# Token scales turned on VectorE, and the residual's way out set back by twelve steps

## The chip, the cores and the metric

The program runs on one core of a Trainium2 chip. The metric is device time in microseconds for one execution of the whole program. The kernel before takes 2173.52 us, the median of three runs from 2171.97 to 2175.43.

## What is computed

Two decoder layers over 256 tokens of width 2048, all in float32. The first mixes tokens with a gated MLP, the second with forgetting attention, whose keys and values come from the residual after the first layer; each is followed by a feed-forward part of width 5632 with a short causal convolution.

```python
def rmsnorm(x, g):
    r = lax.rsqrt(jnp.mean(x * x, axis=-1, keepdims=True) + EPS)
    return (x * r) * g

h = x
h = h + chunked_gmlp(rmsnorm(h, a_norm), a_w_in, a_v_norm, a_w_s, a_b_s, a_w_out)
h = h + conv_ffn(rmsnorm(h, f_norm[0]), f_w_up[0], f_conv_w[0], f_conv_b[0], f_w_down[0])
k, v, c = fox_shared_kv(h, kv_norm, w_kvf, b_f, k_norm)
h = h + forgetting_attention(rmsnorm(h, b_norm), b_w_qg, q_norm, b_w_out, k, v, c)
h = h + conv_ffn(rmsnorm(h, f_norm[1]), f_w_up[1], f_conv_w[1], f_conv_b[1], f_w_down[1])
return rmsnorm(h, final_norm)
```

The factor `r` of each rmsnorm is one number per token. The kernel multiplies the residual by the gain alone, runs the matmul on that, and applies `r` to the product; these 256 factors are the token scales.

## The kernel before

**The weights' way.** Every weight matrix comes from DRAM in chunks of 128 x 1024 floats (512 KB). Class `Stream` loads a chunk into a tile `raw` on SP's queue (line 78), six chunks ahead of its use, and three chunks ahead splits it in two: ScalarE rounds it to `whi` (line 112), VectorE takes the remainder `wlo` (line 113). TensorE then makes three products for each true one: rounded with rounded, remainder with rounded, rounded with remainder. So each operand has a high and a low part; the activations' parts lie in `X1`, `X2` (in the trace `mlp_X` and `att_X`) and `H` (`ffn_H`). All these matmuls stand on line 226, in the helper `mm`.

**Two kinds of blocks.** In a feature block (`feat_block`) the weights are stationary and the activations stream, 256 tokens at a time. In a token block (`tok_blocks`, `seven_block`) the activations are stationary and the weights stream, mostly 256 columns at a time. The trace lists the streamed operand first, so token blocks read `whi,X` and feature blocks `X,whi`. There are four `whi` and four `wlo` tiles in turn, each 1024 + 64 floats long; weights start at the tile's start in feature blocks and 32 floats further in token blocks (`FEAT_AT, TOK_AT = 0, 32`). Two tiles that nothing uses, `spare` of 16 floats and `place` of 144, stand in the pools.

**Steps.** Work beside the matmuls is written as generators. `advance` takes each of them one `yield` further after every chunk that TensorE has been given, so a `yield` is one chunk, and the order on every engine's queue is the order in which this code runs. Nothing reorders it later.

**Token scales.** `token_sums` sums the squares, and `rsqrt` leaves the 256 scales in `rcol`, 128 partitions by 2. For products that have tokens along the free dimension they are also wanted as a row on every partition, `rB`. `token_rows` writes `rcol` to DRAM from GpSimd's queue, one element of four bytes at a time (line 359), and reads the row back to all partitions (line 363). It runs twice: key "a" near the start, in one piece, and key "b" at about 1029 us, in eight pieces each way with two yields after each.

**The residual's way out.** During attention the residual `h` isn't needed, and its place is used by other tiles. `kv_operand` first prepares the operand `att_X2` from `h`, a step for each of 16 parts, and then sends `h` to the DRAM tensor `kept` in eight transfers of 256 KB, one after every two steps (line 1042, on SP's queue, which also carries the weight loads). `heads`, the attention itself, demands that all eight have been issued; its tiles `parts_qk` and `parts_pv` lie where `h` was.

Of the kernel before, what the change touches and what calls it, by code (L numbers as in the profile page):

```python
# [10 lines left out]
F32 = mybir.dt.float32  # L11
# [6 lines left out]
P = 128  # L18
D = 2048
T = 256  # L20
# [168 lines left out]
def build(ctx, tc, d, out):  # L189
    nc = tc.nc  # L190
    ctx.enter_context(tc.manual_schedule())
    const = ctx.enter_context(tc.tile_pool(name="const", bufs=1))
    wpool = ctx.enter_context(tc.tile_pool(name="wpool", bufs=AHEAD + 1))
    small = ctx.enter_context(tc.tile_pool(name="small", bufs=1))
# [8 lines left out]
    X1 = const.tile([P, KD, 2 * T], F32R, name="X1")  # L203
    acc = const.tile([P, T], F32, name="acc")
    rB = const.tile([P, T], F32, name="rB")
    rcol = const.tile([P, 2], F32, name="rcol")
    ident = const.tile([P, P], F32, name="ident")
    ones = const.tile([P, 2], F32, name="ones")

# [8 lines left out]
    def misc_ps():  # L218
        return psum.tile([P, 512], F32, name="mp", tag="mp", bufs=2)

    def column(i):
        return col[:, i:i + 1]
# [99 lines left out]
    def prep(dst, kt, gain):  # L322

        g = column(gain + kt)
        nc.scalar.activation(dst[:, kt, :T], h[:, kt, :], AF.Copy, scale=g)
        nc.vector.scalar_tensor_tensor(dst[:, kt, T:], h[:, kt, :], g, dst[:, kt, :T].bitcast(F32),
                                       op0=OP.mult, op1=OP.subtract)
# [17 lines left out]
    def token_sums():  # L345

        between()
        mp = misc_ps()
        sum_tokens(mp, acc, True, True)
        v = small.tile([P, 2], F32, name="ts_v", tag="ts_v", bufs=2)  # L350
        nc.vector.tensor_scalar(v, mp[:, :2], 1.0 / D, EPS, op0=OP.mult, op1=OP.add)
        rsqrt(rcol, v, 2)

    def token_rows(key, pieces=1):

        way = dram.tile([1, T], F32, name=f"way_r{key}")
        n = P // pieces
        for i in range(0, P, n):
            nc.gpsimd.dma_start(way.rearrange("o (t p) -> p (o t)", t=2)[i:i + n], rcol[i:i + n])
            yield  # L360
            yield
        for i in range(0, P, n):
            nc.gpsimd.dma_start(rB[i:i + n], way[:1, :].to_broadcast([n, T]))
            if n < P:
                yield
                yield

    def token_scale():
        yield
        token_sums()  # L370
        yield
        yield from token_rows("b")
# [338 lines left out]
    def residual_prepared():  # L711

        for p in range(8):
            while state["added"] < 2 * (p // 2 + 1):
                yield
            for kt in (2 * p, 2 * p + 1):
                prep(X1, kt, C_BNORM)
            if p == 5:
                s.start(residual_squares())
            yield  # L720

    def residual_squares():

        for p in range(8):
            while state["added"] < 2 * (p // 2 + 1):
                yield
            sq = small.tile([P, 2, T], F32, name="sq", tag="sq", bufs=2)
            nc.scalar.activation(sq, h[:, 2 * p:2 * p + 2, :], AF.Square)
            yield
            if p == 0:  # L730
                nc.vector.tensor_tensor(acc, sq[:, 0, :], sq[:, 1, :], op=OP.add)
            else:
                for i in range(2):
                    nc.vector.tensor_tensor(acc, acc, sq[:, i, :], op=OP.add)
        yield
        token_sums()
        state["rows"] = True
        yield
        yield from token_rows("b", 8)

    def short_block(src, x, K, done):

# [87 lines left out]
    def warm_up(n):  # L830

        mp = misc_ps()
        for _ in range(n):
            nc.tensor.matmul(mp[:, :P], ident, ident, start=True, stop=True)  # L834

    def input_norm():
        for _ in range(3):
            yield
        for p in range(8):
            if p % 2 == 0:  # L840
                yield
            square_into_acc(p)
        yield
        token_sums()
        state["normed"] = True
        yield
        yield from token_rows("a")
# [148 lines left out]
    def att(key):  # L996
        ph.open("att")
        shape = {"X2": [P, KD, 2 * T], "q": [P, NH, T], "k": [P, 4, 8, 4, 32], "v": [P, 2, D],
                 "ccol": [P, 2, NH], "gain": [P, 1]}[key]
        return ph.keep(key, shape, F32R if key == "X2" else F32)  # L1000
# [29 lines left out]
    def kv_operand():  # L1030
        for _ in range(3):
            yield
        nc.vector.tensor_tensor(att("gain"), column(C_QNORM), column(C_KNORM), op=OP.mult)
        for kt in range(KD):
            while state["added"] < 2 * (kt // 4 + 1):
                yield
            prep(att("X2"), kt, C_KVNORM)
            yield
        for i in range(8):
            yield  # L1040
            yield
            nc.sync.dma_start(kept[:, 2 * i:2 * i + 2, :], h[:, 2 * i:2 * i + 2, :])
        state["kept"] = True

# [250 lines left out]
    def g_done(p):  # L1295
        def done(ps, both):
# [4 lines left out]
            while state["done"] < 2 * p + 2 or state["gates"] < p:  # L1301
# [20 lines left out]
    nc.gpsimd.memset(ident, 1.0)  # L1322
    nc.gpsimd.affine_select(ident, ident, pattern=[[-1, P]], compare_op=OP.is_equal, fill=0.0,
                            base=0, channel_multiplier=1)
    warm_up(9)

    v_blocks = [(d["a_in_v"][8 * blk:8 * blk + 8], v_done(blk)) for blk in range(4)]
# [12 lines left out]
    for blk in range(4):  # L1340
        seven_block(blk, d["down0"][22 * blk:22 * blk + 22], order_of(blk, 2, (8, 4)), *sums_apart(blk))

    s.then(at_mult=lambda: s.start(kv_operand()))
    tok_blocks([(d["b_q"][8 * blk:8 * blk + 8], head_norm("q", blk)) for blk in range(4)], lambda: X1,
               order=[(n, i) for i in range(3) for n in range(6)] + [(6, 0), (7, 0), (0, 3), (1, 3), (6, 1), (7, 1)]
# [89 lines left out]
```

## Time and profile before

| what | value |
|---|---|
| median of three runs | 2173.52 us (2171.97 to 2175.43) |
| the profiled execution | 2175.22 us, granted clock 0.998 |
| its span, from first to last instruction | 2173.5 us |
| DMA engines, by queue | q1 66.0%, q0 0.6%, q8 0.4% of 16 engines' span |
| moved | 455.73 MB, mean 210 GB/s |

The span is what the profile's rows add up to; the 1.7 us around it are start and end of the execution. In the rows below, PE is TensorE, PEld its loading of stationary operands, DVE VectorE, ACT ScalarE, POOL GpSimd, SPq the queue that issues most transfers. A busy TensorE only says that a matmul is in flight; matmuls overlap, so how fast it goes is seen from how many start in a stretch.

### The profile page before, as it was taken

To read this page: it belongs to the slowest core of one execution; us is meant where nothing else is said; L and a number is where in the kernel's file an instruction comes from. 1 tells how busy PE (TensorE), PEld (TensorE's weight loads), DVE (VectorE), ACT (ScalarE), POOL (GpSimd) and SP (SyncE) were. 2 spreads that over 40 slices of the span, in tenths; PEclk is the share of its full clock that TensorE was granted. 3 is DMA by queue.
4 is the path that set the end of the run, shared out by engine and by line. 5 is a ranking of instruction groups with operands and counts; after the bars stand their busy time and mean duration, and the time that the engine had idled before them with its cause. 6 is when DMAs were issued, how large, how long until landed. Compare 5 with 4: busy or idle time off the path is not lost.

```text
span 2173.5 us, 45433 instructions
## 1 busy us (share of the span) xinstructions
PE 2161.4 (99%) x18558; PEld 2145.2 (99%) x18558; DVE 1671.2 (77%) x2448; ACT 1222.2 (56%) x1709; POOL 31.9 (1%) x60
## 2 busy tenths in 40 slices
PE   9999999999999999999999999999999999999998
PEld 9999999999999999999999999999999999999998
DVE  6696687777777799998877886668777777779997
ACT  6665555555555555566445775445555555555555
POOL 0000000000000000000000100000000000000000
PEclk9999999999999999999999999999999999999999
DMA  8686566666666567777977777566866666665665
GB/s 314 191 247 201 192 196 195 187 201 188 200 191 197 183 197 228 220 231 206 256 244 249 238 229 231 187 205 198 267 194 194 190 199 191 198 190 189 204 204 165
DMA packets 161729, 455.73 MB, mean 210 GB/s; under 512 B 26816, under 2 KB 50256, under 8 KB 161136
## 3 DMA queue, kind: packets, MB, share of 16 engines
q1 hardware_dynamic: 159552, 448.87, 66.0%
q0 software_dynamic: 1504, 3.41, 0.6%
q8 instruction: 145, 2.38, 0.4%
q10 hardware_dynamic: 464, 0.55, 0.1%
q14 instruction: 64, 0.52, 0.1%
HBM read 434.91 MB, written 17.84 MB: 208 GB/s over the span
## 4 chain that ended last, share of the span: by engine, by line
PE 96%; DMA 2%; DVE 1%; SPq 0%; ACT 0%; issue 0%; POOL 0%; DVEq 0%; ACTq 0%; POOLq 0%
PE ps L226 94%; PE mp L226 1%; DMA raw<-b_q 1%; DMA att_rows<-way_q 0%; DMA way_q<-att_turned 0%; DVE wlo L113 0%; DMA raw<-kvf_k 0%; DMA raw<-kvf_ks 0%; SPq L1014 0%; PE mp L834 0%; PE mp L1282 0%; PE ps L1279 0%; ACT whi L112 0%; ACT sq L459 0%; DVE h_h L801 0%
## 5 line engine op out<-in xcount | busy, mean ns | idle before, releaser
L113 DVE TENSOR_TENSOR wlo<-raw,whi 128x1024 fp32r<-128x1024 f32 (+1 forms) x724 | 878.8, 1219 | 262.3 <-ACT whi L112 258.4
L112 ACT ACTIVATE whi<-raw 128x1024 fp32r<-128x1024 f32 (+1 forms) x724 | 762.0, 1057 | 554.5 <-PE ps L226 432.4
L226 PE MATMUL ps<-X,whi 128*128 128x256 f32 (+1 forms) x6466 | 823.7, 280 | 0.0
L226 PEld LDWEIGHTS ps<-X,whi 128*128 128x128 f32 x6466 | 775.3, 188 | 6.8
L226 PE MATMUL ps<-X,wlo 128*128 128x256 f32 x3328 | 445.0, 276 | 0.0
L226 PEld LDWEIGHTS ps<-X,wlo 128*128 128x128 f32 x3328 | 409.7, 188 | 1.7
L226 PE MATMUL ps<-whi,ffn_H 128*128 128x256 f32 (+1 forms) x2124 | 347.1, 277 | 0.0
L226 PEld LDWEIGHTS ps<-whi,ffn_H 128*128 128x128 f32 x2124 | 292.8, 188 | 0.7
L226 PE MATMUL ps<-wlo,ffn_H 128*128 128x256 f32 (+1 forms) x1060 | 220.6, 277 | 0.0
L226 PE MATMUL ps<-whi,X 128*128 128x256 f32 (+1 forms) x1272 | 213.7, 279 | 0.0
L226 PEld LDWEIGHTS ps<-whi,X 128*128 128x128 f32 x1272 | 180.4, 188 | 1.3
L226 PE MATMUL ps<-whi,att_X 128*128 128x256 f32 (+2 forms) x970 | 169.6, 290 | 2.0 <-ACT whi L112 2.0
L978 DVE SCALAR_TENSOR_TENSOR ffn_room<-ffn_room,col 128x255 f32<-128x255 f32 x352 | 161.9, 481 | 6.4
L226 PEld LDWEIGHTS ps<-wlo,ffn_H 128*128 128x128 f32 x1060 | 165.7, 188 | 0.2
L226 PEld LDWEIGHTS ps<-whi,att_X 128*128 128x128 f32 x970 | 139.8, 190 | 5.5 <-ACT whi L112 2.2
L226 PE MATMUL ps<-wlo,X 128*128 128x256 f32 (+1 forms) x634 | 140.6, 279 | 0.0
L410 DVE TENSOR_TENSOR ffn_room<-ps,rB 128x512 f32<-128x512 f32 x76 | 52.5, 691 | 114.2 <-PE ps L226 114.1
L974 ACT ACTIVATE ffn_room<-ffn_room,col 128x256 f32<-128x256 f32 x176 | 96.3, 594 | 53.4 <-DVE ffn_room L410 53.4
L226 PE MATMUL ps<-wlo,att_X 128*128 128x256 f32 (+2 forms) x476 | 108.4, 292 | 0.9 <-DVE wlo L113 0.8
L226 PEld LDWEIGHTS ps<-wlo,X 128*128 128x128 f32 x634 | 102.6, 188 | 0.4
L90 ACT ACTIVATE whi<-raw 128x768 fp32r<-128x768 f32 x54 | 45.8, 848 | 79.6 <-PE ps L226 58.7
L90 ACT ACTIVATE whi<-ffn_room 128x512 fp32r<-128x512 f32 x108 | 64.3, 627 | 32.1 <-PE ps L226 18.9
(237 smaller groups left out, 1692.9 us busy)
## 6 DMA issues: line engine op xcount, KB each, us to landing
raw<-up SPq DMA_DIRECT2D x352, 512.0 KB, 4.2
raw<-down SPq DMA_DIRECT2D x176, 512.0 KB, 4.3
raw<-a_in_u SPq DMA_DIRECT2D x32, 512.0 KB, 4.5
raw<-a_out SPq DMA_DIRECT2D x32, 512.0 KB, 4.1
raw<-b_q SPq DMA_DIRECT2D x32, 512.0 KB, 4.6
raw<-kvf_v SPq DMA_DIRECT2D x32, 512.0 KB, 5.1
raw<-b_g SPq DMA_DIRECT2D x32, 512.0 KB, 4.0
raw<-b_out SPq DMA_DIRECT2D x32, 512.0 KB, 4.3
```

What stands on the lines that cost most here:

```text
L90: self.nc.scalar.activation(hi[:, cols], src[:, cols], AF.Copy)
L112: self.nc.scalar.activation(h, raw, AF.Copy)
L113: self.nc.vector.tensor_tensor(l, raw, h.bitcast(F32), op=OP.subtract)
L226: nc.tensor.matmul(o, a, b, start=start, stop=stop, skip_group_check=True)
L410: nc.vector.tensor_tensor(a, src, rB[:, None, :].to_broadcast([P, 2, T]), op=OP.mult)
L974: nc.scalar.activation(c[:, m, :], a[:, m, :], AF.Identity, scale=w[2], bias=column(C_CONVB + l * 2 * KF + f))
L978: nc.vector.scalar_tensor_tensor(c[:, m, n:], a[:, m, :T - n], w[k], c[:, m, n:], op0=OP.mult, op1=OP.add)
```

## The change

`rcol` becomes the first two columns of a tile `scales` of 128 x 32, which GpSimd sets to zero at the start. VectorE turns it in blocks of 32 x 32 into a new tile `turned_r`, so that in each block the 32 scales of a token half lie in one partition, behind each other. Four transfers of 2 x 32 floats take them to DRAM, and one transfer brings the row back to all partitions. For key "b" that is 1 + 2 yields in place of 32. And `kv_operand` waits twelve more steps before the residual goes out, with three steps instead of two before each transfer.

```diff
-    rcol = const.tile([P, 2], F32, name="rcol")
+    scales = const.tile([P, 32], F32, name="scales")
+    rcol = scales[:, :2]
...
-    def token_rows(key, pieces=1):
+    def token_rows(key):
 
         way = dram.tile([1, T], F32, name=f"way_r{key}")
-        n = P // pieces
-        for i in range(0, P, n):
-            nc.gpsimd.dma_start(way.rearrange("o (t p) -> p (o t)", t=2)[i:i + n], rcol[i:i + n])
-            yield
-            yield
-        for i in range(0, P, n):
-            nc.gpsimd.dma_start(rB[i:i + n], way[:1, :].to_broadcast([n, T]))
-            if n < P:
-                yield
-                yield
+        turned = small.tile([P, 32], F32, name="turned_r", tag="turned_r")
+        nc.vector.transpose(turned, scales)
+        yield
+        for g in range(4):
+            nc.gpsimd.dma_start(way.rearrange("o (t g i) -> (o t) g i", t=2, g=4)[:, g, :],
+                                turned[32 * g:32 * g + 2, :])
+        yield
+        yield
+        nc.gpsimd.dma_start(rB, way[:1, :].to_broadcast([P, T]))
...
-        yield from token_rows("b", 8)
+        yield from token_rows("b")
...
             prep(att("X2"), kt, C_KVNORM)
             yield
+        for _ in range(12):
+            yield
         for i in range(8):
-            yield
-            yield
+            for _ in range(3):
+                yield
             nc.sync.dma_start(kept[:, 2 * i:2 * i + 2, :], h[:, 2 * i:2 * i + 2, :])
...
+    nc.gpsimd.memset(scales, 0.0)
     warm_up(9)
```

**The order on GpSimd's queue.** The scales' transfers stand between the mask of the mixing weights (`mlp_wT`) and the attention's rows (`att_cB`). Before:

```order
L1323 AFFINE_SELECT ident<-ident 128x128
L863 AFFINE_SELECT mlp_wT<-mlp_wT 128x2048
L359 DMA way_ra<-rcol 128x2x1
L363 DMA rB<-way_ra 128x256
L359 DMA way_rb<-rcol 16x2x1 x8
L363 DMA rB<-way_rb 16x256 x8
L1170 MEMSET att_big 16x256
```

After:

```order
L1325 AFFINE_SELECT ident<-ident 128x128
L1327 MEMSET scales 128x32
L863 AFFINE_SELECT mlp_wT<-mlp_wT 128x2048
L362 DMA way_ra<-turned_r 2x32 x4
L366 DMA rB<-way_ra 128x256
L362 DMA way_rb<-turned_r 2x32 x4
L366 DMA rB<-way_rb 128x256
L1172 MEMSET att_big 16x256
```

One transfer of 256 elements and eight of 32 have become four of two rows each, twice; the eight transfers back are one.

**The order on SP's queue**, in the last part of the queries' weights (`b_q`) and the first of the keys' (`kvf_ks`); `way_q` and `att_rows` are the queries' own exchange through DRAM. Before, from the first `kept` on:

```order
L1042 DMA kept<-h_h 128x512
L78 DMA raw<-b_q 128x1024
L1014 DMA way_q_13071<-att_turned 32x4x128 x4
L78 DMA raw<-b_q 128x1024
L1042 DMA kept<-h_h 128x512
L1014 DMA way_q_13107<-att_turned 32x4x128 x4
L78 DMA raw<-b_q 128x1024
L1018 DMA att_rows<-way_q_13071 128x512
L78 DMA raw<-b_q 128x1024
L1042 DMA kept<-h_h 128x512
```

After, `kept` is gone from that place and begins behind the fifth of the six loads that carry the forget gate (`kvf_fk`):

```order
L78 DMA raw<-kvf_fk 128x544
L1044 DMA kept<-h_h 128x512
L1018 DMA att_rows<-way_q_13496 128x512
L1014 DMA way_q_13575<-att_turned 32x4x128 x4
L78 DMA raw<-kvf_fk 128x544
L1014 DMA way_q_13610<-att_turned 32x4x128 x4
L78 DMA raw<-kvf_k 128x1024
L1018 DMA att_rows<-way_q_13575 128x512
L78 DMA raw<-kvf_k 128x1024
L1044 DMA kept<-h_h 128x512
L1018 DMA att_rows<-way_q_13610 128x512
```

The eight transfers have moved from among the loads of `b_q`, `kvf_ks` and `kvf_fk` to among those of `kvf_fk` and `kvf_k`. On TensorE and ScalarE no instruction moves; VectorE has the two transposes more, each one chunk behind the last step of `rsqrt`.

**Where the tiles lie.** A pool's tiles lie behind each other in every partition, in the order in which the code asks for them, at multiples of 32 bytes, and a pool behind the one before it. `scales` takes 128 bytes where `rcol` took 32, and `turned_r` 128 more in the pool `small`. So all that lies behind moves. In bytes from a partition's start, in the built programs:

| tile | before | after |
|---|---|---|
| X1 | 7520 | 7520 |
| whi, first of four (each 4352 = 17 x 256 behind the last) | 42912 | 43008 |
| wlo, first of four | 60320 | 60416 |
| ones_r, sq (first) | 94688, 94752 | 94784, 94848 |
| mlp_X2, and later H of both layers | 99168 | 99392 |
| att_X2 | 119680 | 119904 |
| mlp_wr, mlp_vr | 164768, 168864 | 164992, 169088 |
| parts_qk, stationary and streamed | 217056, 219104 | 217056, 219104 |

For the matmuls on line 226, where the streamed operand starts less where the stationary one does, as a remainder by 256 (offsets within the tiles are multiples of 256, but for the 128 bytes of `TOK_AT`):

| pair | before | after |
|---|---|---|
| X1 with whi or wlo, feature / token blocks | 192 / 192 | 96 / 32 |
| mlp_X2, feature blocks | 192 | 64 |
| H, token blocks | 192 | 64 |
| att_X2, feature / token blocks | 224 / 160 | 96 / 32 |
| parts_qk; mlp_vr with mlp_wr | 0; 0 | 0; 0 |
| sq with ones_r | 64 | 64 |

## The prediction

> **What bounds the kernel now.** I read the page's busy shares first, then TensorE's waits, then its matmuls grouped by operand and shape, then counts of matmuls in stretches where only one pair of operands runs.
>
> ```profile
> span 2173.5 us, 45433 instructions
> PE 2161.4 (99%) x18558; PEld 2145.2 (99%) x18558; DVE 1671.2 (77%) x2448; ACT 1222.2 (56%) x1709; POOL 31.9 (1%) x60
> ...
> PE ps L226 <- ACT whi L112: 2.0, 1, 2.0
> PE mp L834 <- POOL ident L1323: 1.5, 1, 1.5
> PE ps L226 <- DVE wlo L113: 0.8, 1, 0.8
> ```
>
> TensorE is busy for 99% of the span and has three waits in all, one of them the start. So the time is the number of matmuls times the step from one start to the next, plus one hole of 2.0 + 0.8 us. Another engine matters only if it opens a new hole. Whatever changes the step of thousands of matmuls matters far more than any transfer. The step isn't the same everywhere:
>
> ```profile
> 300.00:360.00 60.00, 60.00 (x532) 1.00 0.67 209
> 1380.00:1440.00 60.00, 60.00 (x510) 1.00 0.56 182
> 900.00:960.00 60.00, 60.00 (x532) 1.00 0.71 223
> 1110.00:1150.00 40.00, 40.00 (x339) 1.00 0.78 248
> 1031.00:1069.00 38.00, 38.00 (x338) 1.00 0.96 226
> ```
>
> These rows give a stretch, TensorE's busy time, the matmuls that touch it, the granted clock (full in all five) and the DMA share. One matmul of about 0.28 us overlaps the next ones, so the step is (stretch + 0.28) / count. Feature blocks: 113.3 ns with X1 (300 to 360), 118.2 ns with att_X2 (1380 to 1440). Token blocks: 113.3 ns with H (900 to 960), 113.2 with X1 (1031 to 1069), 118.8 with att_X2 (1110 to 1150). All run 256 columns at full clock on the same line. The slow feature stretch has the lowest DMA share of the five, the fast X1 token stretch the highest, so traffic doesn't make the difference. The operands do:
>
> ```profile
> L226 PE MATMUL ps<-X,whi 128*128 128x256 f32 x6276 | 776.0, 276 | 0.0
> L226 PE MATMUL ps<-X,wlo 128*128 128x256 f32 x3328 | 445.0, 276 | 0.0
> L226 PE MATMUL ps<-whi,ffn_H 128*128 128x256 f32 x2112 | 343.3, 276 | 0.0
> L226 PE MATMUL ps<-wlo,ffn_H 128*128 128x256 f32 x1052 | 217.5, 276 | 0.0
> L226 PE MATMUL ps<-whi,X 128*128 128x256 f32 x1248 | 206.2, 276 | 0.0
> L226 PE MATMUL ps<-whi,att_X 128*128 128x256 f32 x852 | 139.9, 283 | 2.0 <-ACT whi L112 2.0
> L226 PE MATMUL ps<-wlo,X 128*128 128x256 f32 x620 | 135.2, 276 | 0.0
> L226 PE MATMUL ps<-wlo,att_X 128*128 128x256 f32 x408 | 84.9, 283 | 0.8 <-DVE wlo L113 0.8
> L226 PE MATMUL ps<-att_X,whi 128*128 128x256 f32 x512 | 65.8, 281 | 0.0
> L226 PE MATMUL ps<-mlp_X,whi 128*128 128x256 f32 x512 | 63.2, 276 | 0.0
> ...
> L226 PE MATMUL ps<-att_X,wlo 128*128 128x256 f32 x256 | 35.5, 281 | 0.0
> L226 PE MATMUL ps<-mlp_X,wlo 128*128 128x256 f32 x256 | 34.2, 276 | 0.0
> L226 PE MATMUL mp<-whi,ffn_H 128*128 128x256 f32 x140 | 27.3, 276 | 0.0
> L226 PE MATMUL mp<-whi,X 128*128 128x256 f32 x128 | 20.2, 276 | 0.0
> ...
> L226 PE MATMUL mp<-wlo,ffn_H 128*128 128x256 f32 x70 | 15.4, 276 | 0.0
> ...
> L226 PE MATMUL mp<-wlo,X 128*128 128x256 f32 x64 | 12.4, 276 | 0.0
> ...
> L226 PE MATMUL mp<-parts_qk,parts_qk 128*128 128x256 f32 x48 | 7.1, 283 | 0.0
> L226 PE MATMUL ps<-mlp_vr,mlp_wr 128*128 128x256 f32 x48 | 6.3, 281 | 0.0
> ...
> L226 PE MATMUL mp<-sq,ones_r 128*128 128x256 f32 x4 | 0.8, 281 | 0.0
> ```
>
> The last number before the second bar is the mean duration: 276 ns for X, H and mlp_X2 with weight parts, 281 to 283 for the rest. Put beside the places of the tiles (the table of the change), this splits cleanly. Take where the streamed operand starts less where the stationary one starts, in bytes of a partition, and the remainder by 256. It is **192** for every pair at 276 ns. The slow ones have 224 and 160 (att_X2), 0 (parts_qk, mlp_vr with mlp_wr) and 64 (sq with ones_r). No slow pair has 192. Two operands that each lie as X1 does within 128 bytes (parts_qk, both 96) are slow together, so the distance speaks louder than either place.
>
> **The change part by part.**
>
> *The places.* The wider `scales` and the new `turned_r` push the weight parts by 96 bytes and the phases' tiles by 224, while X1 stays. By the table no pair keeps the remainder 192: X1 gets 96 and 32, H and mlp_X2 get 64, att_X2 96 and 32. The trace shows neither 96 nor 32 over a long stretch, and 64 only in the four sq rows, whose stationary operand is one column read 128 times. Bounds: nothing, if remainders that differ by 128 are alike for H and mlp_X2 and the others happen to be free; 7 ns each, the step from 276 to 283. I take the step of att_X2, the nearest long rows: 118.2 less 113.3 is 4.9 ns in feature blocks, 118.8 less 113.3 is 5.5 in token blocks. Feature blocks, X1: 6276 + 3328 = 9604; mlp_X2: 512 + 256 = 768; together 10372 x 4.9 ns = 50.8 us. Token blocks, X1: 1248 + 620 + 128 + 64 = 2060; H: 2112 + 1052 + 140 + 70 = 3374; together 5434 x 5.5 ns = 29.9 us. **Sum +80.7 us.** att_X2 is slow already and gets nothing. Nothing hides this: TensorE has no idle time to give.
>
> *The turn and the eight rows.* Here the only hole is at stake. The rows are TensorE's timeline, one microsecond of its clock, the chain of work that ended last, the issues of transfers, and three stretches.
>
> ```profile
> 1094.00 0.28 PE L226 MATMUL ps<-whi,att_X 128*128 128x272 f32 x1
> ...
> 1096.31 0.51 PE L226 MATMUL ps<-whi,att_X 128*128 128x256 f32 x2 [2.02 <-ACT whi L112]
> ...
> 1101.79 0.38 PE L1146 MATMUL mp<-ident,att_f 128*16 128x128 f32 x2
> ...
> 1098.00:1099.00 1.00, 1.00 (x6) 0.50 0.67 147
> ...
> 1032.03 14.15 DMA raw<-b_q
> ...
> way_rb<-rcol POOLq DMA_DIRECT2D x8, 0.1 KB, 11.3
> ...
> 1046.00:1092.00 46.00, 45.90 (x391) 45.67 (x391) 38.67 (x76) 24.54 (x30) 3.86 (x8) 1.00 0.94 298
> 1092.00:1145.00 53.00, 50.23 (x398) 49.33 (x397) 42.70 (x84) 25.80 (x32) 0.30 (x1) 0.97 0.78 250
> 1030.00:1046.00 16.00, 16.00 (x143) 16.00 (x142) 9.67 (x22) 6.00 (x8) 3.21 (x7) 1.00 0.95 112
> ```
>
> From 1094.12 to 1101.79, 7.67 us, 24 products run (the rows between are two, four, two and so on), which take 24 x 118 ns = 2.83 us at the usual step: the hole costs **4.8 us**, the wait and then some 3.3 us at clock 0.50. Its cause stands in the lower rows: while the 256 single elements go out (11.3 us to landing, median), the engines are 0.95 busy and move 112 GB/s, a b_q load takes 14.15 us, and the next stretch runs at 298 GB/s without catching up. After the change four transfers of two 128-byte rows do the same. I take the whole hole as gone: **-4.8 us**; bounds 0 and -4.8. Two transposes of 128x32 on VectorE (77% busy) and one memset on the idle GpSimd at the start I set at nothing: no matmul waits for rB, and TensorE's cover is the three split chunks ahead.
>
> *The residual.* Eight transfers of 256 KB on SP's queue leave the stretch up to 1092 for the one behind it. The rows are those that touch `kept`, and the first writer of h's place.
>
> ```profile
> L1042 SPq DMA_DIRECT2D kept<-h_h x8: 319/436/495, 1042.7 to 1085.9; - x8
> L1219 ACT ACTIVATE parts_qk<-att_q x8: 413/420/421, 1171.1 to 1263.3; 128x256 fp32r<-128x256 f32 x8
> ```
>
> Each issue holds SP for 0.4 us and waits for nothing. By the order they go out from about 1082 to 1139 on the old clock, past loads of kvf_fk and kvf_k and the q and k exchanges, which wait 0.4 us each. 2.1 MB over 53 us add 40 GB/s to 250, just under the 298 seen. The place of h is written again from 1171, 32 us later, so that wait stays covered. Cost 0; if the cover is gone, a second hole of at most the first one's 4.8.
>
> The profiled execution took 2175.22 us, 1.7 above its span and 1.7 above the median 2173.52, so span and median agree. 2173.5 + 80.7 - 4.8 = **2249.4**.
>
> **The rivals.**
>
> *Period 128.* If remainders by 128 count, H and mlp_X2 (64 instead of 192) stay fast and X1 alone slows: 9604 x 4.9 + 2060 x 5.5 = 58.4; 2173.5 + 58.4 - 4.8 = 2227.1. For it: all long rows fit as well. Against it: sq with ones_r at 64 takes 281, and the kernel sets weights 128 bytes further in token blocks alone, which would be idle.
>
> *One operand's own place.* If the activations' start by 64 decides (32 good, 0 bad), X1 stays, H and mlp_X2 lose 3374 x 5.5 + 768 x 4.9 = 22.3 and att_X2 gains (852 + 408) x 5.5 + 768 x 4.9 = 10.7: 2173.5 + 22.3 - 10.7 - 4.8 = 2180.3. Against it: parts_qk, mlp_vr and mlp_wr lie at 32 and are slow.
>
> *Faster.* If places don't matter and att_X2 is slow by something else, for instance by its stage, the hole alone goes: 2173.5 - 4.8 = 2168.7. It decides as soon as X1 keeps its 113.3 ns. Against it: X1 in the same stage (1031 to 1069) runs at 113.2. [...]
>
> *The hole stays,* since the residual now loads the stretch of kvf_k: 2249.4 + 4.8 = 2254.2.
>
> **How the numbers follow.** Forecast 0.48, hole stays 0.05, period 128 0.27, own place 0.06, places free 0.14. The forecast's own range, with steps 1 ns to either side on 15806 matmuls, is 2234 to 2265. With period 128 it reaches down to 2217 (0.9 us per 1000 matmuls on 11664). 2217 to 2265 leaves out own place and places free, 0.20. Anything under 4.3 us, 0.2%, can't be told from no change: 2168.7 lies just beyond it, so its 0.14 splits into faster 0.08 and same 0.06. Slower 0.86.
>
> **What would show it.** The same rows by operand and shape: 281 to 283 for X, H and mlp_X2 as for att_X2 is the forecast; 276 for H and mlp_X2 period 128; 276 everywhere the faster rival. No wait for whi or wlo near 1094 shows the hole gone; way_rb landing in some 2 to 4 us its cause. If X runs at 276, the prediction is wrong at its largest term.

## The result and the profile after

| what | before | after |
|---|---|---|
| median of 5 runs each | 2174.19 us (2171.97 to 2175.43) | 2257.77 us (2257.24 to 2258.63) |
| ratio | | 1.0386, interval 1.0371 to 1.0401 |
| the profiled execution | 2175.22 us, span 2173.5 | 2257.24 us, span 2255.5 |

The kernel became 3.9% slower. The busy shares on the page of the changed kernel:

```profile
span 2255.5 us, 45422 instructions
PE 2245.9 (100%) x18558; PEld 2229.8 (99%) x18558; DVE 1674.1 (74%) x2450; ACT 1222.6 (54%) x1709; POOL 28.0 (1%) x53
```

TensorE's waits in the changed kernel (who waits, for whom; us in all, times, longest):

```profile
PE mp L834 <- POOL ident L1325: 1.5, 1, 1.5
PE mp L1148 <- ACT att_f L1143: 0.5, 1, 0.5
```

The same 18558 matmuls keep TensorE busy for 84.5 us longer, while it waits less: the hole for `whi` and `wlo` is gone, and a wait of 0.5 us has come for `att_f`, the forget gates, which ScalarE takes from PSUM just before TensorE turns them (1143.7 us). So all that was lost lies in the step from one matmul to the next. Stretches of the changed kernel with one pair each (from:to in us, TensorE's busy time and matmuls, granted clock, DMA share, GB/s), in this order: X1 feature, att_X2 feature, H token, att_X2 token, X1 token, mlp_X2 feature:

```profile
320.00:380.00 60.00, 60.00 (x502) 1.00 0.62 189
1425.00:1485.00 60.00, 60.00 (x502) 1.00 0.56 179
940.00:1000.00 60.00, 60.00 (x512) 1.00 0.67 212
1152.00:1188.00 36.00, 36.00 (x311) 1.00 0.85 267
1076.00:1110.00 34.00, 34.00 (x291) 1.00 0.77 232
205.00:245.00 40.00, 40.00 (x355) 1.00 0.57 187
```

The clock is full in all six. X1 in feature blocks gets 502 matmuls into 60 us where it had 532. Its step, (60 + 0.28) / 502, is 120.1 ns, and so is that of att_X2. H has 117.7, att_X2 in token blocks 116.7, X1 in token blocks 117.8; mlp_X2 has 40.28 / 355 = 113.5 and lost nothing. The groups by operand and shape (busy us, mean ns of one) say the same:

```profile
L227 PE MATMUL ps<-X,whi 128*128 128x256 f32 x6276 | 817.2, 282 | 0.0
L227 PE MATMUL ps<-X,wlo 128*128 128x256 f32 x3328 | 466.7, 282 | 0.0
L227 PE MATMUL ps<-whi,ffn_H 128*128 128x256 f32 x2112 | 353.0, 279 | 0.0
L227 PE MATMUL ps<-wlo,ffn_H 128*128 128x256 f32 x1052 | 221.4, 279 | 0.0
L227 PE MATMUL ps<-whi,X 128*128 128x256 f32 x1248 | 211.6, 280 | 0.0
L227 PE MATMUL ps<-whi,att_X 128*128 128x256 f32 x852 | 137.3, 279 | 0.0
...
L227 PE MATMUL ps<-att_X,whi 128*128 128x256 f32 x512 | 66.6, 282 | 0.0
L227 PE MATMUL ps<-mlp_X,whi 128*128 128x256 f32 x512 | 63.2, 276 | 0.0
```

What the change was made of is seen in the issues of transfers between 1060 and 1200 us (KB each, median us to landing):

```profile
kept<-h_h SPq DMA_DIRECT2D x8, 256.0 KB, 5.7
rB<-way_rb POOLq DMA_DIRECT2D x1, 128.0 KB, 3.9
way_rb<-turned_r POOLq DMA_DIRECT2D x4, 0.2 KB, 3.6
```

and in the stretches from 1069 us on (now with all five engines ahead of clock, DMA share and GB/s). The scales go out and come back in the first one, from 1075.8 to about 1085 us:

```profile
1069.00:1085.00 16.00, 16.00 (x128) 15.55 (x128) 11.16 (x25) 8.40 (x12) 2.62 (x5) 1.00 0.63 185
1085.00:1101.00 16.00, 16.00 (x138) 16.00 (x137) 14.48 (x37) 7.72 (x9) 0.00 (x0) 1.00 0.70 206
1101.00:1147.00 46.00, 45.46 (x371) 44.79 (x370) 33.46 (x60) 25.36 (x36) 0.00 (x0) 1.00 0.86 275
1147.00:1200.00 53.00, 53.00 (x445) 52.43 (x444) 47.58 (x102) 23.84 (x26) 1.38 (x3) 1.00 0.79 246
```

The rows land in 3.6 us where the elements took 11.3, and the stretch that holds them is 0.63 busy at 185 GB/s, where that of the elements was 0.95 busy at 112.

### The profile page after: what moved, and what is told of

Same layout as the page of the kernel before. It is cut to its first block, busy times and chain, and to the rows that moved or that the text cites. A ratio compares the mean times of both kernels' runs of the same rounds, so it can differ in the third digit from the quotient of the medians.

```text
span 2255.5 us, 45422 instructions
## 1 busy us (share of the span) xinstructions
PE 2245.9 (100%) x18558; PEld 2229.8 (99%) x18558; DVE 1674.1 (74%) x2450; ACT 1222.6 (54%) x1709; POOL 28.0 (1%) x53
## 4 chain that ended last, share of the span: by engine, by line
PE 97%; DMA 1%; DVE 1%; ACT 0%; issue 0%; SPq 0%; DVEq 0%; POOL 0%; ACTq 0%; POOLq 0%
PE ps L227 95%; PE mp L227 1%; DVE wlo L113 0%; DMA raw<-kvf_k 0%; DMA raw<-kvf_fk 0%; DMA way_q<-att_turned 0%; DMA raw<-b_q 0%; PE mp L834 0%; ACT whi L112 0%; PE mp L1284 0%; PE ps L1281 0%; DVE att_big L1104 0%; ACT sq L1093 0%; DVE att_turned L1007 0%; DVE att_hv L1095 0%
## 5 line engine op out<-in xcount | busy, mean ns | idle before, releaser
L227 PE MATMUL ps<-X,whi 128*128 128x256 f32 (+1 forms) x6466 | 865.0, 285 | 0.0
L227 PEld LDWEIGHTS ps<-X,whi 128*128 128x128 f32 x6466 | 815.4, 188 | 7.0
L227 PE MATMUL ps<-X,wlo 128*128 128x256 f32 x3328 | 466.7, 282 | 0.0
L227 PEld LDWEIGHTS ps<-X,wlo 128*128 128x128 f32 x3328 | 429.4, 188 | 1.7
L227 PE MATMUL ps<-whi,ffn_H 128*128 128x256 f32 (+1 forms) x2124 | 356.8, 280 | 0.0
L227 PEld LDWEIGHTS ps<-whi,ffn_H 128*128 128x128 f32 x2124 | 299.1, 188 | 0.7
L227 PE MATMUL ps<-whi,X 128*128 128x256 f32 (+1 forms) x1272 | 219.4, 282 | 0.0
```

Of the source, the lines that this page charges most:

```text
L227: nc.tensor.matmul(o, a, b, start=start, stop=stop, skip_group_check=True)
```

## The experiments

The theory is the prediction's: the distance between the starts of the two operands, as a remainder by 256 bytes, sets the step, and the rest of the change removes the hole. Rivals are that the new instructions and transfers cost something themselves, that an operand's own place decides, and that distances 128 apart are alike. Below, "distance" is this remainder. A ratio with its interval comes from several rounds; the other kernels were run once.

### The change, with every tile at its old place

```diff
-    scales = const.tile([P, 32], F32, name="scales")
-    rcol = scales[:, :2]
+    const.tile([P, 2], F32, name="gap")
...
-    small.tile([P, 144], F32, name="place")
+    scales = small.tile([P, 32], F32, name="scales")
+    rcol = scales[:, :2]
+    turned = small.tile([P, 32], F32, name="turned_r")
+    small.tile([P, 80], F32, name="place")
...
-        turned = small.tile([P, 32], F32, name="turned_r", tag="turned_r")
```

(against the changed kernel; the new tiles take a part of `place`, which nothing used)

> The whole change, but `scales` and `turned_r` take their room from the unused tile `place`, so that every tile lies at the byte where it lay before. Theory (the distance of the two operands sets the matmul's step): 276 ns again for X1 and H, the step back at 113.4 ns, and the hole near 1094 us gone: 2174.2 - 4.8 = 2169.4, within 1.5. Rival (the new transposes, transfers or the residual's new place slow TensorE): near 2257.

2170.42 us against 2175.01 before: ratio 0.9981, interval 0.9972 to 0.9989. Its groups by operand and shape:

```profile
L229 PE MATMUL ps<-X,whi 128*128 128x256 f32 x6276 | 776.0, 276 | 0.0
L229 PE MATMUL ps<-whi,ffn_H 128*128 128x256 f32 x2112 | 343.4, 276 | 0.0
...
L229 PE MATMUL ps<-whi,att_X 128*128 128x256 f32 x852 | 138.6, 281 | 0.0
```

Its three stretches, beside those that the prediction shows of before:

```profile
1030.00:1046.00 16.00, 16.00 (x144) 16.00 (x143) 12.04 (x27) 7.98 (x11) 2.62 (x5) 1.00 0.63 181
1046.00:1092.00 46.00, 46.00 (x395) 46.00 (x394) 37.57 (x75) 24.75 (x31) 0.00 (x0) 1.00 0.89 274
1092.00:1145.00 53.00, 53.00 (x439) 52.51 (x438) 45.66 (x95) 26.50 (x33) 0.30 (x1) 1.00 0.83 273
```

All that the change says it does is here, and it gains 4.6 us. TensorE gets 439 matmuls into the last stretch instead of 398, 41 x 118 ns = 4.8 us of work, and is busy for all of it; its only wait left in the whole span is the start's 1.5 us. The loss isn't in the work.

### The places alone

```diff
-    rcol = const.tile([P, 2], F32, name="rcol")
+    rcol = const.tile([P, 32], F32, name="rcol")[:, :2]
...
         way = dram.tile([1, T], F32, name=f"way_r{key}")
+        if key == "a":
+            small.tile([P, 32], F32, name="unused")
```

(against before: no instruction is added, removed or moved in order; every tile lies where the change puts it)

> The kernel before, with `rcol` asked for at 128 bytes and an unused tile of 128 bytes in `small`, so that every tile lies where it lies in the changed kernel; no instruction differs. Theory: the steps of the changed kernel, 120.0 (X1 feature), 117.3 (X1 token), 117.8 (H): 2174.2 + 86 = 2260, and down to 2255 if the hole closes because the b_q chunks last longer. Rival: 2174.

2260.12 us: ratio 1.0397, interval 1.0383 to 1.0411. By operand and shape:

```profile
L226 PE MATMUL ps<-X,whi 128*128 128x256 f32 x6276 | 817.1, 282 | 0.0
L226 PE MATMUL ps<-whi,ffn_H 128*128 128x256 f32 x2112 | 353.0, 279 | 0.0
...
L226 PE MATMUL ps<-mlp_X,whi 128*128 128x256 f32 x512 | 63.2, 276 | 0.0
```

The 248 bytes of each partition that nobody reads (120 behind `rcol`, 128 of `unused`) are the whole loss. These three rows repeat those of the changed kernel to 0.1 us of busy time, the fast mlp_X2 too, so the step isn't chance from run to run. TensorE shows no wait for `whi` or `wlo` here though the single elements still go out. That fits a longer step, at which it asks for fewer weights in the same time; no run tests it. In place of the hole it waits for `att_f`, longer than the changed kernel does:

```profile
PE mp L1148 <- ACT att_f L1143: 1.9, 1, 1.9
```

### The rows alone, and the residual's delay alone

The first is the kernel of "every tile at its old place" with the residual's old steps; the second is before with the new ones.

```diff
-        for _ in range(12):
-            yield
         for i in range(8):
-            for _ in range(3):
-                yield
+            yield
+            yield
```

> The turned scales and the eight rows alone, the residual's way out as before, every tile at its old byte. If the 256 elements make the hole, no wait near 1094 us and 2169.4, within 1.5. If the residual's eight transfers make it, the wait stays: 2174, within 1.5.

> The residual's later way out alone, the scales as elements as before, every tile at its old byte. If the 256 elements make the hole, it stays at least in part: 2171 to 2174. If the residual makes it, it is gone: 2169.4.

The rows alone: 2170.64 us, ratio 0.9979, interval 0.997 to 0.9988. The delay alone: 2174.59 us, ratio 0.9998, interval 0.999 to 1.0007. The stretch of the scales with the rows alone, and then with the delay alone:

```profile
1030.00:1046.00 16.00, 16.00 (x140) 15.87 (x139) 12.01 (x28) 8.33 (x10) 2.62 (x5) 1.00 0.62 179
```

```profile
1030.00:1046.00 16.00, 16.00 (x143) 16.00 (x143) 9.44 (x22) 5.77 (x8) 2.99 (x7) 1.00 1.00 108
```

The rows free the DMA engines, 0.62 busy at 179 GB/s where before has 0.95 at 112; the delay doesn't: with it they are busy all the time and move 108 GB/s. TensorE's waits with the delay alone:

```profile
PE mp L834 <- POOL ident L1325: 1.5, 1, 1.5
PE mp L1148 <- ACT att_f L1143: 1.3, 1, 1.3
PE mp L226 <- DVE wlo L113: 0.8, 1, 0.8
```

The delay alone lies just above the 2171 to 2174 that was expected if the elements make the hole. The hole of 2.0 us for `whi` is gone from the profiled execution, the waits that it has lie elsewhere (`wlo` at 1049.6 us, `att_f` at 1099.0), and its clock stays full there (1.00 from 1046 to 1145 us). But it took 2172.49 us, 2.1 under the median, and the median doesn't move. The eleven runs spread over 6.6 us (2171.5 to 2178.06), those of the rows alone over 2.6 (2169.39 to 2172.03). That fits a cover so thin that waits come and go from one execution to the next while the single elements remain; only one execution is profiled, so this stays a reading. The rows take the whole gain, and the delay adds nothing to them (2170.42 with both).

### Which distance, and how it counts

Four kernels shift weights or everything. Against before, the first three change the line of the weights' offsets (in floats, so 32 is 128 bytes), the fourth widens `spare`, which lies ahead of everything named here:

```diff
-FEAT_AT, TOK_AT = 0, 32
+FEAT_AT, TOK_AT = 32, 0
```

```diff
-FEAT_AT, TOK_AT = 0, 32
+FEAT_AT, TOK_AT = 16, 16
```

```diff
-FEAT_AT, TOK_AT = 0, 32
+FEAT_AT, TOK_AT = 48, 48
```

```diff
-    const.tile([P, 16], F32, name="spare")
+    const.tile([P, 24], F32, name="spare")
```

For X1, mlp_X2 and H the distance becomes 64, 128, 0 and, in the fourth, stays 192 with every tile 32 bytes further.

> The kernel before with FEAT_AT, TOK_AT = 32, 0: weight parts start 128 bytes later in feature blocks and 128 earlier in token blocks, all else in place. Remainders by 256: X1 and mlp_X2 in feature blocks 64, X1 and H in token blocks 64, att_X2 96 and 32. If only the distance by 256 counts, read from the changed kernel: feature blocks stay at 113.4 ns (276), token blocks go to 117.8 (279): 5480 x 4.4 ns = 24 us more, 2198. If a period of 128 holds for token blocks too: 276 everywhere and 2174. If H was slow in the changed kernel for its own place (0 by 64): 276 here, for X1 and H have not moved.

> The kernel before with FEAT_AT, TOK_AT = 16, 16: remainders 128 for X1, mlp_X2 and H in both kinds of blocks, att_X2 160 and 96. Neither has been seen. Distance theory: no remainder but 192 (and 64 in feature blocks) has been fast, so 279 to 283 and a step of 116 to 121: 2174 + 17500 x 3 to 7 ns = 2220 to 2290. Rival (only steps that are no multiple of 64 collide): 276 and 2174.

> The kernel before with FEAT_AT, TOK_AT = 48, 48: remainder 0 for X1, mlp_X2 and H in both kinds of blocks, att_X2 32 and 224. Distance theory, read from parts_qk and mlp_vr at 0 (281 to 283, steps 118 to 120): 17500 x 5 to 7 ns = 2255 to 2290. If those were slow for being short runs: 276 and 2174.

> The kernel before with 8 floats more in the unused tile `spare`: X1, all weight parts and all tiles behind them lie 32 bytes further, every distance on line 226 as before (192, and 224 and 160 for att_X2). Distance theory: 2174, every group at its old duration. Rival (an operand's own place by 64 or 128 decides): X1, whi and H change together, by tens of us.

Measured, one run each: 2241.26, 2256.68, 2273.65 and 2176.8 us, against 2177.12 for one run of before. The row of X1 with `whi` in feature blocks, at distance 64, 128, 0 and 192 (a fence for each kernel):

```profile
L226 PE MATMUL ps<-X,whi 128*128 128x256 f32 x6276 | 801.4, 279 | 0.0
```

```profile
L226 PE MATMUL ps<-X,whi 128*128 128x256 f32 x6276 | 809.4, 281 | 0.0
```

```profile
L226 PE MATMUL ps<-X,whi 128*128 128x256 f32 x6276 | 817.4, 283 | 0.0
```

```profile
L226 PE MATMUL ps<-X,whi 128*128 128x256 f32 x6276 | 776.1, 276 | 0.0
```

Of these four, 192 alone gives 276 ns. Shifting everything together by 32 bytes changes nothing, so the distance counts and not the place (a shift by 224 bytes follows below). 64, 128 and 0 all differ from 192 and from each other, so the period isn't 128. The first kernel was a **miss**: since mlp_X2 had kept 276 ns at distance 64 in the changed kernel, feature blocks were expected to run at 276 and the kernel near 2198; they ran at 279, mlp_X2 with them.

### Why mlp_X2 kept its step

Two tries at the fast mlp_X2 of the changed kernel. The first is the kernel with offsets 32 and 0 again, with `spare` widened so that mlp_X2 lies exactly where the change puts it; the second moves only the tiles of the phases, by 128 bytes:

```diff
-    const.tile([P, 16], F32, name="spare")
+    const.tile([P, 72], F32, name="spare")
```

```diff
-    small.tile([P, 144], F32, name="place")
+    small.tile([P, 176], F32, name="place")
```

> e5_at_32_0 with `spare` 224 bytes longer: all distances as there (64 for X1, mlp_X2 and H in both kinds of blocks), but in feature blocks the streamed operand now starts at 64 and the stationary one at 0 by 256, as mlp_X2 did in the changed kernel, where it kept 276. If the own places decide at distance 64: X1 and mlp_X2 at 276 in feature blocks, some 10372 x 4.2 ns = 43 us under e5_at_32_0, 2198. If they don't: 279 and 2241, and mlp_X2 in the changed kernel stays unexplained.

> The kernel before with 32 floats more in the unused tile `place`: X1 and the weight parts stay (192 throughout), the phases' tiles lie 128 bytes further: mlp_X2 and H at 64, att_X2 at 96 and 32. H: 279 as wherever token blocks had 64, att_X2 282 and 280: 2174 + 3422 x 4.4 ns = 2189. The open pair is mlp_X2 at 64, which comes here behind fast X1 products. If what ran before it sets its regime (276 behind X1 at 96, 279 behind X1 at 64), 276 or 279 here adds a third case; if distance 64 is slow whenever weights and activations don't both start at a multiple of 64 bytes, 279, and 768 x 4.4 ns = 3 us more.

The first took 2241.11 us, as without the shift by 224 bytes (2241.26), with mlp_X2 at 279 ns: its own place doesn't explain it. The second took 2180.39 (before, one run: 2175.28), where 2189 and 3 us more were expected: a **miss**. mlp_X2 at distance 64 was slow here too. But H, at 64 as well, came to 277 in the mean, and stretches of the first layer show why:

```profile
765.00:800.00 35.00, 35.00 (x299) 1.00 0.67 194
820.00:855.00 35.00, 35.00 (x312) 1.00 0.73 225
```

35.28 / 299 is 118.0 ns, 35.28 / 312 is 113.1. One pair at one distance has **two regimes**, and the same trace changes from one to the other. The timeline shows where:

```profile
807.92 0.28 PE L226 MATMUL ps<-whi,ffn_H 128*128 128x256 f32 x1
808.03 0.28 PE L226 MATMUL ps<-whi,X 128*128 128x256 f32 x1
...
809.41 0.28 PE L226 MATMUL ps<-whi,ffn_H 128*128 128x256 f32 x1
```

From 759.7 to 808.0 us 410 products of H follow each other, at 117.8 ns. Then come twelve of X1 (distance 192), and all of H behind them runs at 113.3. In the second layer the same happens at 1989.9 us. The kernel with offsets 32 and 0 has both regimes as well, for X1 in feature blocks:

```profile
1356.00:1400.00 44.00, 44.00 (x391) 1.00 0.79 251
1530.00:1640.00 110.00, 110.00 (x937) 1.00 0.74 230
```

That is 113.2 and 117.7 ns; ahead of either stretch stand products of 512 columns. In none of the five traces that have a pair at 64 (the changed kernel, the places alone, and the kernels with offsets 32 and 0, with and without the wider `spare`, and with the wider `place`) does the regime change within an unbroken run of eight or more such products. That fits a choice in which what ran just ahead has a part, but its speed alone doesn't decide: mlp_X2 ran fast behind X1 at 96 (120 ns, the changed kernel) and slow behind X1 at 192 (113 ns, here). No run varies this by itself, and which regime comes can't be foretold from these traces.

### The last slow operand put right

The kernel of "every tile at its old place", with 224 unused bytes ahead of att_X2, which brings it from 224 and 160 to 192:

```diff
+        if key == "X2":
+            ph.keep("before_x2", [P, 56])
         return ph.keep(key, shape, F32R if key == "X2" else F32)
```

> e1_same_places, and an unused tile of 224 bytes ahead of att_X2, so that its remainders too are 192 in feature and token blocks; everything else on line 226 but the short runs (parts, mlp_vr, sq) has 192 already. Distance theory: att_X2's 2000 long products go from 118.3 and 118.7 to 113.4: 768 x 4.9 + 1260 x 5.3 ns = 10.4 us less than e1_same_places: 2160, within 2, 0.7% under the kernel before. If att_X2 was slow by its stage: 2170.

2162.18 us against 2174.68: ratio 0.9944, interval 0.993 to 0.9957. Its rows for att_X2:

```profile
L229 PE MATMUL ps<-whi,att_X 128*128 128x256 f32 x852 | 134.2, 276 | 0.0
...
L229 PE MATMUL ps<-att_X,whi 128*128 128x256 f32 x512 | 63.2, 276 | 0.0
```

The rule foretold the step of an operand that had always been slow: 281 became 276. The time is just outside the 2160 within 2 that was expected. The gain over the kernel without the unused bytes is 8.2 us (two chips, whose medians of before differ by 0.3) instead of 10.4. The steps did what was foretold: start to start over the two traces, 768 x 5.0 + 1260 x 5.1 ns = 10.3. A part went to a wait that the profile of the kernel without the unused bytes doesn't have:

```profile
PE mp L1151 <- ACT att_f L1146: 1.1, 1, 1.1
```

The rest, about 1 us, stays open. This version beats both kernels.

### The distances together

Steps in ns from the starts of the matmuls in the traces, 256 columns at full clock:

| distance | step | where |
|---|---|---|
| 192 | 113.3 to 113.6 | X1, H, mlp_X2 before; att_X2 in the last kernel |
| 64 | 117.8, or 113.3 | H after; mlp_X2 after (the two regimes) |
| 32 | 117.1 to 117.8 | X1 and att_X2 after and with the places alone, token blocks; att_X2 with offsets 48, 48, feature blocks |
| 160 | 117.3, 118.7 | att_X2 with offsets 16, 16, feature blocks; att_X2 before, token blocks |
| 224 | 118.3 | att_X2 before, feature blocks |
| 128 | 118.7 | X1 and H with offsets 16, 16 |
| 0 | 119.95 | X1 and H with offsets 48, 48 |
| 96 | 120.0 | X1 and att_X2 after, feature blocks |

## Why the prediction came out

The time, 2257.77, lies in the range and 8.4 us above the number. Its steps:

**What bounds the kernel.** Held. TensorE's idle time in the span fell from 12.1 to 9.6 us and the kernel still became 3.9% slower.

**The distance.** Held. The places alone cost 1.0397, the rest of the change 0.9981.

**The size of the step.** Here the terms were off, and the range held partly by luck. The step of att_X2 before, at 224 and 160, stood in for distances no long row had shown. X1 in feature blocks, now at 96, lost 120.1 - 113.3 = 6.8 ns where 4.9 was taken: 65.3 us by these stretches instead of the 47.1 that 9604 of the 10372 made. One matmul more or less in a stretch is 0.24 ns there, 2.3 us; start to start over the trace it is 6.6 ns, 63.4 us. mlp_X2 lost nothing instead of 3.8 us. Token blocks lost less than 5.5 ns: X1 117.8 - 113.2 = 4.6 on 2060, H 117.7 - 113.3 = 4.4 on 3374, together 24.3 instead of 29.9. att_X2 went to other distances, 1.9 ns slower on 768 and 2.1 faster on 1260: -1.2 instead of 0. The sum, 65.3 + 24.3 - 1.2 = 88.4, less the hole's 4.8 is 83.6, against 82.0 between the spans. With starts over the whole trace for every pair it is 63.4 + 8.2 (X1, token) + 14.9 (H) + 1.3 - 2.0 (att_X2) = 85.8, less the hole 81.0. So errors partly cancelled: the X1 feature step, too small by 16 to 18 us, outweighed mlp_X2, the token blocks and att_X2, which were too large by 3.8, 5.6 and 1.2. The range allowed 1 ns to either side of each step; X1 in feature blocks lay 1.9 off and mlp_X2 4.9 the other way.

**The turn and the rows.** Held but for the new wait of 0.5 us for `att_f`: 3.6 us to landing, no wait for `whi` or `wlo`, and 4.4 us gained by the rows alone, near the 4.8 (interval of its ratio: 0.12 to 0.30%, 2.6 to 6.5 us). The transposes took 0.2 us each, and TensorE waited for neither.

**The residual.** Held at 0. From the changed kernel, the issues and the first writer of h's place (ns min, median, max; first and last start):

```profile
L1044 SPq DMA_DIRECT2D kept<-h_h x8: 320/426/648, 1125.2 to 1182.3; - x8
...
L1221 ACT ACTIVATE parts_qk<-att_q x8: 407/420/421, 1212.1 to 1303.4; 128x256 fp32r<-128x256 f32 x8
```

The last goes out 30 us ahead of the first writer, the new stretch moves 246 to 275 GB/s, and no wait for weights opened there.

**The rivals.** Period 128 falls with H at 279 ns after and with distance 64 for all (279 ns, 2241.26 us); that mlp_X2 stayed fast, as that rival had it, fits the faster of the two regimes at 64. Own place falls with the kernel shifted by 32 bytes, where X1 starts at 0 by 64 and still takes 276 ns. Places free falls with the places alone: 2260.12 us, where it has 2168.7. The hole that stays falls with TensorE's waits in the changed kernel: none for `whi` or `wlo`.

## What to carry to other kernels

In this kernel, whose TensorE is busy for 99% of the span, two small tiles between the operands made the steps of X1 and H 4.0 to 6.6 ns longer; 32 bytes ahead of both operands changed nothing (2176.8 us against 2177.12). So where TensorE is the bound, compare the addresses of the built programs, not the diff alone. Where a measured step differs between operands of one shape, put their distance beside it; here 224 unused bytes ahead of att_X2 were worth 0.4% (2162.18 us against 2170.42), and losing the distance cost 4% (2260.12 against 2175.01). Carve new small tiles out of padding that is there, or put them ahead of or behind all operands, and judge the intended edit with the places held.

## What was not expected of the hardware

- The step has more than a good and a bad value: 113.3 to 113.6 ns at distance 192, and at the other seven from 117.1 to 120.0 (at 64 at times 113.3). All these are products of 256 columns. At 512 little of it shows: X1 with `whi` took 396 ns before, 397 after, and 394 to 397 in the other kernels (190 matmuls in each).
- At distance 64 the same pair runs at 118.0 or 113.1 ns, and the choice repeats: at the same place in both layers, and for mlp_X2 in two kernels with the same places. It changes only where other products stand between. Whether those make the choice, and why the distance counts at all, stays open: no run here shows it.
- The places alone took the hole for the weights away as well, at 3.97% more time. A wait that vanishes from the profile is no gain by itself.
- The clock doesn't fall behind every hole. Before, the granted clock was 0.50 for some 3.3 us behind waits of 2.0 and 0.8 us. In the kernel shifted by 32 bytes the waits at the same place were 2.5 and 0.7 us, and the clock stayed full behind them:

```profile
PE ps L226 <- ACT whi L112: 2.5, 1, 2.5
...
1100.00:1101.00 1.00, 1.00 (x8) 1.00 0.53 139
1101.00:1102.00 1.00, 1.00 (x11) 1.00 0.68 193
```

So the 4.8 us are what the hole cost in one execution of before. The 3.3 us at clock 0.50 in it are missing in the kernel shifted by 32 bytes.
